# Grouped-query values as eight full-width fp32r products on high and low parts, with the evictions of a step in another order

## The chip, the cores and the metric

The kernel runs on one core of a Trainium2 chip. The metric is the device time of one execution in microseconds; lower is better. All inputs and outputs are float32.

## The reference

One layer of an encoder on 512 tokens of width 1024. Three token mixers work on the same projection of x: neighbourhood attention, grouped-query attention (8 query heads of width 64, 2 key and value heads, each shared by four query heads) and attention into 256 memory tokens. Their outputs are gated, projected, summed and normalised; a mixture of 16 experts follows. What the change touches is the grouped-query branch:

```python
def block(qi):
    s = jnp.einsum('bkgqd,bskd->bkgqs', qi, k, preferred_element_type=jnp.float32) * scale
    p = jax.nn.softmax(s, axis=-1)
    return jnp.einsum('bkgqs,bskd->bqkgd', p.astype(v.dtype), v)
```

for each of four blocks of 128 queries, over all 512 keys.

## The kernel before

In the trace an fp32 product leaves two records, an fp32r product or a transpose one. Where the kernel wants fp32r speed and more than fp32r's precision it splits an operand x into hi = cast(x) and lo = x − hi (`hi_lo`, L99 to L101: a cast on ScalarE, then a subtraction on VectorE that waits for it) and sums the products of the parts. All projection weights go through this: a unit of 128x1024 is loaded, cast (tiles `whi` or `los`) and subtracted (`los`), two units ahead of its use (`Stream.prefetch`).

The grouped-query attention is cut into 16 units: 4 pairs of heads (`hp`) by 4 blocks of 128 tokens (`m`), class `GqaUnit` (L627). A unit goes through five phases:

- `S`: scores of two heads into two PSUM banks (`gs`), two fp32r products each.
- `soft` and `norm`: per head the negated maximum (VectorE), the exponential with its sum (ScalarE); then the reciprocal of the sums and two multiplications (VectorE). The probabilities lie in `att_twin`, two buffers.
- `T`: eight fp32 transposes of 128x128 into two banks (`gt`).
- `tev`: the transposed probabilities go back to SBUF, one copy on VectorE and one on ScalarE.
- `PV`: the values (`gy`), for each of 4 key chunks and 2 heads an fp32 product whose stationary operand is 128x64 of `vg` (the value projection) and whose moving operand is 128 columns. The two heads write the two halves of the partitions, so they lie in different 64-column tiles of the array.
- `yev`: the result is split by `hi_lo` into `yg`.

`Attn.step` (L778) runs three units at once, in this order on each engine:

```python
u.S(); a.T(); b.PV()
u.soft(); a.tev(); u.norm(); b.yev()
```

with u the newest unit, a the one before and b the one before that. On TensorE the transposes of unit a thus stand right behind the scores of unit u and need a's normalisation, which was issued a step earlier. The banks: two for scores, two for transposes, one for values, and three (tag `mm`) that all projections share.

Steps are woven into the projections by `run`: after each piece of a projection one step is issued, then one entry of the background list `bg`, then the eviction of the piece. In the stretch at hand the pieces are the gates of the memory branch (`gate_piece`, 24 products of 512 columns, evicted by a tanh on ScalarE), its projection (`proj_piece`, 12 products, tile `pr`, evicted on VectorE into `macc`) and the neighbourhood values (`nv`, two steps for each of four chunks). `bg` holds the rotary embedding of the queries (`rope_stages`, L386): a square on ScalarE, sums and a reciprocal root on VectorE (L401, L402, L104 to L109), two multiplications (L406, L407), four operations on GpSimd, and transposes of the queries (`rT`) with a cast and a subtraction for each head (`qs`, L446, L447). Engines work in order: what waits holds back all that is queued behind it on that engine.

Of the kernel before, what the change touches and what calls it, by code (L numbers as in the profile page):

```python
# [10 lines left out]
F32R = mybir.dt.float32r  # L11
# [7 lines left out]
P = 128  # L19
# [53 lines left out]
def layer_kernel(ctx: ExitStack, tc: tile.TileContext, xt, xn, first0, wu, bgate, rpb, gains, wrt,  # L73
# [260 lines left out]
    ST = {}  # L334

    def g_mem():
        zz = R("Q3", [P, 4, 1024], "mkvzs")
# [116 lines left out]
    def g_gqa():  # L454
# [3 lines left out]
        b1t = b01[:, 2:4]  # L458
        vg = b1t[:, 0, :512].rearrange("p (m f) -> p m f", m=NT)
        ST.update(khh=kk[:, 0:2], klo=kk[:, 2:4], vg=vg, qs=(qs[:, 0:4], qs[:, 4:8]),  # L460
                  rope=(vs_t[:, 0], b1t[:, 1]), zr=b01[:, 0:2])
        rope = []
        for q in range(3):
            us = ws.take(2)
            zs = ST["A5" if q % 2 else "A6"][:, 1, :512 if q == 0 else 1024].rearrange("p (m c) -> p m c", m=NT)
            for m in range(NT):
                acc = PB("mm", f"gq{q}{m}")
                n_chunk(acc[:, :256], us, xh, xl, m)
                ws.prefetch(2 if m == NT - 1 else 1)
                yield  # L470
                if q == 0:
                    nc.scalar.copy(zs[:, m], acc[:, :P])
                    nc.scalar.copy(vg[:, m], acc[:, P:256])
                else:
                    nc.scalar.copy(zs[:, m], acc[:, :256])
            rope.append(rope_stages(q, zs, 2 if q == 0 else 4, 1 if q == 0 else 0))
            bg.extend(rope[q] if q == 0 else rope[q][:4] if q == 1 else [])
# [105 lines left out]
    class MemUnit:  # L583
# [38 lines left out]
        def yev(self):  # L622
            yh, yl = ST["y2"]
            d = (slice(None), slice(2 * self.hp, 2 * self.hp + 2), slice(self.m * P, (self.m + 1) * P))
            hi_lo(yh[d], yl[d], self.y)

    class GqaUnit:  # L627
        def __init__(self, hp, m):
            self.hp, self.m = hp, m

        def S(self):
# [9 lines left out]

        def soft(self):
            self.p = twin("P").rearrange("p (h c) -> p h c", h=2)
            self.sm = small([P, 2], "sm")
            nm = small([P, 2], "nm")
            for h in range(2):
                nc.vector.tensor_reduce(nm[:, h:h + 1], self.s[h], axis=AX.X, op=ALU.max, negate=True)  # L647
                nc.scalar.activation(self.p[:, h], self.s[h], AF.Exp, bias=nm[:, h:h + 1],  # L648
                                     accum_out=self.sm[:, h:h + 1])

        def norm(self):
            recip_norm(self.p, self.sm, lambda h: self.p[:, h])

# [8 lines left out]
        def tev(self):  # L662
            self.pt = twin("PT").rearrange("p (h k c) -> p h k c", h=2, k=4)
            nc.vector.tensor_copy(self.pt[:, 0], self.t[0])
            nc.scalar.copy(self.pt[:, 1], self.t[1])

        def PV(self):
            self.y = PB("Y", f"gy{self.hp}{self.m}")
            kvh = self.hp // 2
            for kc in range(4):  # L670
                for h in range(2):
                    nc.tensor.matmul(self.y[h * 64:h * 64 + 64, :P], ST["vg"][:, kc, kvh * 64:kvh * 64 + 64],
                                     self.pt[:, h, kc], start=(kc == 0), stop=(kc == 3))

        def yev(self):
            yh, yl = ST["y1"]
            d = (slice(None), self.hp, slice(self.m * P, (self.m + 1) * P))
            hi_lo(yh[d], yl[d], self.y[:, :P])

# [89 lines left out]
    class Attn:  # L769
# [7 lines left out]
        def step(self):  # L777
# [8 lines left out]
            if b:  # L786
                b.PV()
            if u:
                u.soft()
# [4 lines left out]
            if b:  # L794
                b.yev()
            self.pipe = [u, a]
            return True

# [89 lines left out]
    run(g_gqa(), 0.85)  # L888
    at.drain()
    dump("ymh", ST["y2"][0].bitcast(F32))  # L890
    yg = R("Q2", [P, 8, S], "yg", F32R)
# [992 lines left out]
```

## Time and profile before

| what | value |
|---|---|
| median of 3 runs | 959.69 us (959.56 to 962.3) |
| the profiled execution | span 958.0 us from the first to the last instruction; the median of the runs is 1.69 us above it |
| TensorE (PE) busy | 934.3 us, 98% |
| VectorE (DVE) busy | 440.3 us, 46% |
| ScalarE (ACT) busy | 285.8 us, 30% |
| GpSimd (POOL) busy | 97.3 us, 10% |
| granted TensorE clock | 1.00 in the stretches looked at |
| DMA | 251.18 MB, mean 262 GB/s |

The table's busy times are shares of a run with several stages. PE is pipelined: a matmul's record lasts longer than the distance to the next one's start, so the cost of a product is read from starts, not from durations. The same holds, to a lesser degree, for consecutive operations on DVE and ACT.

### The profile page before, as it was taken

The page shows a single profiled execution, that of the slowest core. Times are in us where ns is not written, and L with a number is a line of the kernel's source. Part 1 is how long each engine was busy: PE and PEld are TensorE (multiplying, and loading weights), DVE is VectorE, ACT ScalarE, POOL GpSimd, SP SyncE. Part 2 cuts the span into 40 slices and gives each one's busy share as a digit, 9 for nine tenths or more (in the row PEclk, how much of TensorE's full clock was granted, in tenths as well). Part 3 has the DMA queues.
Part 4 walks back from the last instruction along what each step waited for, and adds up shares of the span by engine and source line. Part 5 has one row for each costly group of instructions (what it writes and reads, how often), then busy time and mean ns, then how long its engine had stood idle before and what let it go on. Part 6 is the DMA issues. An engine that isn't in the chain of part 4 may idle for free. (4 is left out here: it accounts for less than half of the span.)

```text
span 958.0 us, 12971 instructions
## 1 busy us (share of the span) xinstructions
PE 934.3 (98%) x5258; PEld 609.5 (64%) x5258; DVE 440.3 (46%) x840; ACT 285.8 (30%) x560; POOL 97.3 (10%) x112
## 2 busy tenths in 40 slices
PE   9999999999999999999999999999999998998997
PEld 9899878888888888888886433533353333533335
DVE  6347668764376567237464111563232222322426
ACT  6334453543344454333232111110110100110123
POOL 0102303000122231000024004000000000000004
PEclk9999999999999999999999999999999999999999
DMA  9322221211433322566929999999999999999992
GB/s 361 115 67 67 66 67 44 67 47 65 116 85 110 103 83 66 199 252 262 382 73 384 427 423 426 427 433 428 432 429 430 432 428 433 430 430 432 428 422 115
DMA packets 40807, 251.18 MB, mean 262 GB/s; under 512 B 13198, under 2 KB 13582, under 8 KB 25516
## 3 DMA queue, kind: packets, MB, share of 16 engines
q1 hardware_dynamic: 40604, 250.10, 65.1%
q8 instruction: 41, 0.67, 0.3%
q10 hardware_dynamic: 144, 0.26, 0.1%
q14 instruction: 18, 0.15, 0.0%
HBM read 247.46 MB, written 2.10 MB: 260 GB/s over the span
## 5 line engine op out<-in xcount | busy, mean ns | idle before, releaser
L1322 PE MATMUL g<-w,xs 128*64 128x512 f32 x508 | 132.6, 600 | 10.3 <-DMA w<-in_wx 10.2
L1322 PE MATMUL u<-w,xs 128*64 128x512 f32 x508 | 130.6, 592 | 0.0
L1358 PE MATMUL y<-w,hT 128*64 128x512 f32 x480 | 106.0, 593 | 0.0
L1322 PEld LDWEIGHTS u<-w,xs 128*64 128x64 f32 x508 | 36.5, 137 | 72.5 <-issue 72.2
L101 DVE TENSOR_TENSOR y<-y,y 64x512 fp32r<-64x512 f32 x28 | 19.3, 689 | 135.0 <-ACT y L100 135.0
L1322 PEld LDWEIGHTS g<-w,xs 128*64 128x64 f32 x508 | 32.9, 136 | 74.7 <-issue 52.6
L101 DVE TENSOR_TENSOR los<-raw_twin,whi 128x1024 fp32r<-128x1024 f32 x42 | 53.6, 1278 | 57.9 <-ACT whi L100 57.7
L1358 PEld LDWEIGHTS y<-w,hT 128*64 128x64 f32 x480 | 34.2, 137 | 68.1 <-issue 65.1
L286 PE MATMUL gate<-xh,los 128*128 128x512 f32 x192 | 74.9, 390 | 0.0
L1454 DVE TENSOR_TENSOR acc<-acc,cb 128x512 f32<-128x512 f32 x56 | 34.7, 681 | 56.6 <-PE cb L1452 56.6
L284 PE MATMUL gate<-xh,whi 128*128 128x512 f32 x144 | 57.2, 397 | 0.0
L285 PE MATMUL gate<-xl,whi 128*128 128x512 f32 x144 | 56.1, 390 | 0.0
L100 ACT CAST y<-y 64x512 fp32r<-64x512 f32 x28 | 16.2, 579 | 130.5 <-PE y L1358 120.0
L100 ACT CAST whi<-raw_twin 128x1024 fp32r<-128x1024 f32 x42 | 44.1, 1050 | 10.0 <-PE wo L1120 6.5
L1534 POOL TENSOR_TENSOR acc<-acc,ln2g 128x512 f32<-128x512 f32 x8 | 10.0, 1273 | 353.2 <-ACT y L100 352.8
L286 PEld LDWEIGHTS gate<-xh,los 128*128 128x128 f32 x192 | 36.0, 188 | 7.7
L648 ACT ACTIVATE att_twin<-gs,nm 128x512 f32<-128x512 f32 x32 | 21.7, 684 | 49.9 <-DVE nm L647 49.9
L1333 DVE SCALAR_TENSOR_TENSOR tg<-tg,g 128x512 f32<-128x512 f32 x16 | 11.0, 687 | 53.4 <-ACT tg L1332 53.4
L1345 ACT COPY hT<-ht 128x512 f32<-128x512 f32 x15 | 8.8, 586 | 89.2 <-PE ht L1340 89.2
L1332 ACT ACTIVATE tg<-g 128x512 f32<-128x512 f32 x16 | 9.6, 597 | 83.5 <-PE g L1322 78.1
L101 DVE TENSOR_TENSOR los<-raw_twin,los 128x1024 fp32r<-128x1024 f32 x20 | 25.0, 1248 | 19.6 <-ACT los L100 19.5
L284 PEld LDWEIGHTS gate<-xh,whi 128*128 128x128 f32 x144 | 27.0, 188 | 6.6 <-issue 1.2
(458 smaller groups left out, 1898.3 us busy)
## 6 DMA issues: line engine op xcount, KB each, us to landing
w<-in_wx SPq DMA_DIRECT2D x74, 2048.0 KB
w<-in_wx SPq DMA_DIRECT2D x43, 1024.0 KB
raw_twin<-in_wu SPq DMA_DIRECT2D x65, 512.0 KB
raw<-in_wu SPq DMA_DIRECT2D x8, 512.0 KB
xr<-in_xt SPq DMA_DIRECT2D x4, 512.0 KB
macc<-in_xn SPq DMA_DIRECT2D x2, 1024.0 KB
out<-acc SPq DMA_DIRECT2D x7, 256.0 KB
first<-in_first SPq DMA_DIRECT2D x4, 384.0 KB
```

The lines of the kernel that those rows point to most:

```text
L100: nc.scalar.copy(hi, src)
L101: nc.vector.tensor_tensor(lo, src, hi.bitcast(F32), op=ALU.subtract)
L284: nc.tensor.matmul(acc, w_h, rh[:, k], start=(k == 0), stop=False)
L285: nc.tensor.matmul(acc, w_h, rl[:, k], start=False, stop=False)
L286: nc.tensor.matmul(acc, w_l, rh[:, k], start=False, stop=(k == nk - 1))
L648: nc.scalar.activation(self.p[:, h], self.s[h], AF.Exp, bias=nm[:, h:h + 1], accum_out=self.sm[:, h:h + 1])
L1322: nc.tensor.matmul(GU[e][b][hf * 64:hf * 64 + 64], xs, w[b][hf] if isinstance(w[b], list) else w[b][:, hf * 512:hf * 512 + 512], start=(k ...
L1332: nc.scalar.activation(th, g, AF.Tanh, scale=0.5)
L1333: nc.vector.scalar_tensor_tensor(th, th, 1.0, g, op0=ALU.add, op1=ALU.mult)
L1358: nc.tensor.matmul(y[o * 64:o * 64 + 64], hT[:, c, hf * 64:hf * 64 + 64], w[j][:, o * 512:(o + 1) * 512], start=(k == 0 and j == 0), stop= ...
L1454: nc.vector.tensor_tensor(a, a, cb, op=ALU.add)
L1534: nc.gpsimd.tensor_tensor(x, x, g2[:, None, quarters[q]].to_broadcast([P, 2, 256]), op=ALU.mult)
```

## The change

1. `vg` becomes fp32r with a high and a low part side by side: 64 columns of high and 64 of low for each value head and key chunk, in a tile of its own (tag `gb`). The value projection's copy becomes a `hi_lo`.
2. `tev` writes the transposed probabilities as a high and a low part (`gpt`, in place of the twin buffers): two casts on ScalarE and two subtractions on VectorE, in place of one copy on each.
3. `PV` is eight fp32r products: 4 key chunks by high and low probabilities, the stationary operand 128x128 (both parts of the values), the moving one 256 columns (both heads). Partitions 0 to 63 of the result hold what the high values give, 64 to 127 what the low values give.
4. `low` is new: ScalarE copies the lower half (64x256) to SBUF (`glow`), VectorE adds it to the upper half, head by head, into spare columns of the same bank. `yev` reads these.
5. `norm` moves one of the two multiplications to ScalarE (a Copy with a per-partition scale), and both for the first pair of heads (hp 0).
6. The probabilities have one buffer in place of two. For grouped-query units the order behind the products is now: maxima of u, casts of a, first exponential of u, low part of b, second exponential and normalisation of u, eviction of b. The other units keep theirs.

```diff
-        vg = b1t[:, 0, :512].rearrange("p (m f) -> p m f", m=NT)
+        vg = R("gb", [P, NT, 2, 2, 64], "vg", F32R)
...
-                    nc.scalar.copy(vg[:, m], acc[:, P:256])
+                    hi_lo(vg[:, m, :, 0], vg[:, m, :, 1], acc[:, P:256].rearrange("p (g f) -> p g f", g=2))
...
+    GQ = {}
+
     class GqaUnit:
...
+            if not GQ:
+                GQ["p"] = ST["b01"][:, 2]
+                GQ["pt"] = R("Q7", [P, 2, 2, 1024], "gpt", F32R)
+                GQ["low"] = R("bf", [P, 3, 256], "glow")
+            self.i = m
...
-        def soft(self):
...
+        def top(self):
+            self.nm = small([P, 2], "nm")
             for h in range(2):
-                nc.vector.tensor_reduce(nm[:, h:h + 1], self.s[h], axis=AX.X, op=ALU.max, negate=True)
-                nc.scalar.activation(self.p[:, h], self.s[h], AF.Exp, bias=nm[:, h:h + 1],
-                                     accum_out=self.sm[:, h:h + 1])
+                nc.vector.tensor_reduce(self.nm[:, h:h + 1], self.s[h], axis=AX.X, op=ALU.max, negate=True)
+
+        def exp(self, h):
...
+            nc.scalar.activation(self.p[:, h], self.s[h], AF.Exp, bias=self.nm[:, h:h + 1],
+                                 accum_out=self.sm[:, h:h + 1])
 
         def norm(self):
-            recip_norm(self.p, self.sm, lambda h: self.p[:, h])
+            rc = small([P, 2], "rc")
+            nc.vector.reciprocal(rc, self.sm)
+            for h in range(2):
+                if h or not self.hp:
+                    nc.scalar.activation(self.p[:, h], self.p[:, h], AF.Copy, scale=rc[:, h:h + 1])
+                else:
+                    nc.vector.tensor_scalar(self.p[:, h], self.p[:, h], rc[:, h:h + 1], None, op0=ALU.mult)
...
         def tev(self):
-            self.pt = twin("PT").rearrange("p (h k c) -> p h k c", h=2, k=4)
-            nc.vector.tensor_copy(self.pt[:, 0], self.t[0])
-            nc.scalar.copy(self.pt[:, 1], self.t[1])
+            self.pt = [GQ["pt"][:, self.i % 2, j].rearrange("p (h k c) -> p h k c", h=2, k=4) for j in range(2)]
+            for h in range(2):
+                hi_lo(self.pt[0][:, h], self.pt[1][:, h], self.t[h])
 
         def PV(self):
-            self.y = PB("Y", f"gy{self.hp}{self.m}")
-            kvh = self.hp // 2
+            y = PB("Y", f"gy{self.hp}{self.m}", (P, 4, P))
+            self.y = y[:, :2]
+            self.ys = y[:, 2]
             for kc in range(4):
-                for h in range(2):
-                    nc.tensor.matmul(self.y[h * 64:h * 64 + 64, :P], ST["vg"][:, kc, kvh * 64:kvh * 64 + 64],
-                                     self.pt[:, h, kc], start=(kc == 0), stop=(kc == 3))
+                v = ST["vg"][:, kc, self.hp // 2].rearrange("p a f -> p (a f)")
+                for j in range(2):
+                    nc.tensor.matmul(self.y, v, self.pt[j][:, :, kc], start=(kc == 0 and j == 0), stop=(kc == 3 and j == 1))
+
+        def low(self):
+            low = GQ["low"][64:, self.i % 3].rearrange("p (h c) -> p h c", h=2)
+            nc.scalar.copy(low, self.y[64:])
+            for h in range(2):
+                nc.vector.tensor_tensor(self.ys[h * 64:h * 64 + 64], self.y[:64, h], low[:, h], op=ALU.add)
...
-            hi_lo(yh[d], yl[d], self.y[:, :P])
+            hi_lo(yh[d], yl[d], self.ys)
+
+        @staticmethod
+        def behind(u, a, b):
+            if u:
+                u.top()
+            if a:
+                a.tev()
+            if u:
+                u.exp(0)
+            if b:
+                b.low()
+            if u:
+                u.exp(1)
+                u.norm()
+            if b:
+                b.yev()
```

Two places of the order that results. The first is ScalarE around a plain step, that of the twelfth unit, with the tanh and the weight cast that stand ahead of it (`gs` are scores, `gt` transposed probabilities, `gy` values). Before:

```order
L505 ACTIVATE th_1807<-gate_1812,consts 128x512
L100 CAST whi_1877<-raw_twin 128x1024
L648 ACTIVATE att_twin,sm<-gs_1894,nm 128x512
L648 ACTIVATE att_twin,sm<-gs_1897,nm 128x512
L665 COPY att_twin<-gt_1905 128x512
L100 CAST yg<-gy_1910 128x128
```

and with the change:

```order
L510 ACTIVATE th_1856<-gate_1861,consts 128x512
L100 CAST whi_1931<-raw_twin 128x1024
L100 CAST gpt<-gt_1954 128x512
L100 CAST gpt<-gt_1959 128x512
L663 ACTIVATE ropevg,sm<-gs_1948,nm 128x512
L699 COPY glow<-gy_1964 64x256
L663 ACTIVATE ropevg,sm<-gs_1951,nm 128x512
L671 ACTIVATE ropevg<-ropevg,rc 128x512
L100 CAST yg<-gy_1964 128x128
```

The two casts come ahead of the exponentials, the low copy between them, and a normalisation stands between the second exponential and the cast of `yg`.

The second is VectorE in the step of the third unit, ahead of the rotary sums (`ss`). Before:

```order
L101 TENSOR_TENSOR los<-raw_twin,whi_1269 128x1024
L647 TENSOR_REDUCE nm<-gs_1298 128x1
L647 TENSOR_REDUCE nm<-gs_1301 128x1
L664 COPY att_twin<-gt_1304 128x512
L579 RECIPROCAL rc<-sm 128x2
L581 TENSOR_SCALAR att_twin<-att_twin,rc 128x512 x2
L101 TENSOR_TENSOR yg<-gy_1314,yg 128x128
L401 TENSOR_REDUCE ss_1072<-ropesq 128x16
```

and with the change:

```order
L101 TENSOR_TENSOR los<-raw_twin,whi_1278 128x1024
L657 TENSOR_REDUCE nm<-gs_1307 128x1
L657 TENSOR_REDUCE nm<-gs_1310 128x1
L101 TENSOR_TENSOR gpt<-gt_1313,gpt 128x512
L101 TENSOR_TENSOR gpt<-gt_1318,gpt 128x512
L701 TENSOR_TENSOR gy_1323<-gy_1323,glow 64x128 x2
L668 RECIPROCAL rc<-sm 128x2
L101 TENSOR_TENSOR yg<-gy_1323,yg 128x128
L406 TENSOR_REDUCE ss_1077<-ropesq 128x16
```

Two subtractions replace a copy, two additions stand ahead of the reciprocal, and the two multiplications are gone to ScalarE; the rotary sums still stand behind the subtraction of `yg`. On TensorE the order of products is as before, and the order on GpSimd and on SyncE's queue does not change.

## Rows read from the trace of the kernel before

**Rows 1.** The page's busy times of each engine.

```profile
PE 934.3 (98%) x5258; PEld 609.5 (64%) x5258; DVE 440.3 (46%) x840; ACT 285.8 (30%) x560; POOL 97.3 (10%) x112
```

**Rows 2.** Stretches: length, then PE, PEld, DVE, ACT, POOL busy, clock, DMA share, GB/s.

```profile
124.90:240.70 115.80, 115.80 (x750) 94.73 (x750) 81.24 (x154) 54.07 (x123) 9.44 (x6) 1.00 0.17 55
520.00:958.00 438.00, 419.96 (x2229) 172.93 (x2225) 131.48 (x262) 66.12 (x127) 20.61 (x20) 1.00 0.97 411
```

**Rows 3.** Timeline of PE, a plain step: start, length, engine, line, operation, count.

```profile
202.69 0.39 PE L638 MATMUL gs<-kk,qs 128*128 128x512 f32 x1
...
203.60 1.04 PE L659 MATMUL gt<-ident,att_twin 128*128 128x128 f32 x8
204.57 1.09 PE L672 MATMUL gy<-att_twin,ropevg 128*64 128x128 f32 x16
205.59 0.50 PE L284 MATMUL pr<-ym,los 128*128 128x512 f32 x1
...
208.48 0.39 PE L638 MATMUL gs<-kk,qs 128*128 128x512 f32 x1
```

**Rows 4.** Timeline of PE in the memory stage: transposes, then 256-column fp32r products.

```profile
62.84 0.60 PE L608 MATMUL mt<-ident,att_twin 128*128 128x128 f32 x4
63.19 0.36 PE L306 MATMUL gq<-whi,xh 128*128 128x256 f32 x1
63.39 0.28 PE L307 MATMUL gq<-los,xh 128*128 128x256 f32 x1
63.51 0.28 PE L308 MATMUL gq<-whi,xl 128*128 128x256 f32 x1
```

**Rows 5.** Timeline of ACT in the same plain step.

```profile
204.13 0.69 ACT L648 ACTIVATE att_twin<-gs,nm 128x512 f32<-128x512 f32 x1 [2.18 <-DVE nm L647]
...
204.81 0.68 ACT L648 ACTIVATE att_twin<-gs,nm 128x512 f32<-128x512 f32 x1
...
205.47 0.58 ACT L665 COPY att_twin<-gt 128x512 f32<-128x512 f32 x1
205.94 0.28 ACT L100 CAST yg<-gy 128x128 fp32r<-128x128 f32 x1
```

**Rows 6.** Timeline of DVE in the same plain step.

```profile
203.34 1.29 DVE L647 TENSOR_REDUCE nm<-gs 128x1 f32<-128x512 f32 x2
204.55 0.68 DVE L664 COPY att_twin<-gt 128x512 f32<-128x512 f32 x1
205.61 0.17 DVE L579 RECIPROCAL rc<-sm 128x2 f32<-128x2 f32 x1 [0.38 <-ACT att_twin L648]
205.81 0.88 DVE L581 TENSOR_SCALAR att_twin<-att_twin,rc 128x512 f32<-128x512 f32 x2
206.61 0.28 DVE L101 TENSOR_TENSOR yg<-gy,yg 128x128 fp32r<-128x128 f32 x1
```

**Rows 7.** Group of a Copy with per-partition scale on ACT: total, mean ns, idle before.

```profile
L1581 ACT ACTIVATE acc<-fin,l2y 128x512 f32<-128x512 f32 x4 | 2.5, 684 | 0.8 <-PE fin L1565 0.8
```

**Rows 8.** Timeline of DVE, third and fourth unit, around the rotary sums.

```profile
138.27 1.23 DVE L101 TENSOR_TENSOR los<-raw_twin,whi 128x1024 fp32r<-128x1024 f32 x1 [0.95 <-ACT whi L100]
...
143.14 1.21 DVE L401 TENSOR_REDUCE ss<-ropesq 128x16 f32<-128x1024 f32 x1
...
146.57 1.22 DVE L101 TENSOR_TENSOR los<-raw_twin,whi 128x1024 fp32r<-128x1024 f32 x1
147.71 1.28 DVE L647 TENSOR_REDUCE nm<-gs 128x1 f32<-128x512 f32 x2
...
150.16 0.88 DVE L581 TENSOR_SCALAR att_twin<-att_twin,rc 128x512 f32<-128x512 f32 x2
```

**Rows 9.** Timeline of PE: the transposes that need that normalisation.

```profile
151.52 1.03 PE L659 MATMUL gt<-ident,att_twin 128*128 128x128 f32 x8
```

**Rows 10.** Timeline of DVE: eviction of a projection behind the transposed queries.

```profile
181.74 0.69 DVE L533 SCALAR_TENSOR_TENSOR macc<-th,pr 128x512 f32<-128x512 f32 x1
```

**Rows 11.** Timeline of PE: the gate that uses that eviction's bank.

```profile
182.82 0.50 PE L284 MATMUL gate<-xh,whi 128*128 128x512 f32 x1
```

More of the change, by code (lines that the diff above doesn't have):

```diff
@@ L334, in layer_kernel, with att_anew @@
     ST = {}
+    def att_anew():
+        for k in ("P", "PT"):
+            twins.pop(k, None)
+        att.clear()
     def g_mem():
@@ L640, in S @@
                 self.s.append(s)
-        def soft(self):
-            self.p = twin("P").rearrange("p (h c) -> p h c", h=2)
-            self.sm = small([P, 2], "sm")
-            nm = small([P, 2], "nm")
+        def top(self):
+            self.nm = small([P, 2], "nm")
             for h in range(2):
-                nc.vector.tensor_reduce(nm[:, h:h + 1], self.s[h], axis=AX.X, op=ALU.max, negate=True)
-                nc.scalar.activation(self.p[:, h], self.s[h], AF.Exp, bias=nm[:, h:h + 1],
-                                     accum_out=self.sm[:, h:h + 1])
-        def norm(self):
-            recip_norm(self.p, self.sm, lambda h: self.p[:, h])
+                nc.vector.tensor_reduce(self.nm[:, h:h + 1], self.s[h], axis=AX.X, op=ALU.max, negate=True)
+        def exp(self, h):
+            if not h:
+                self.p = GQ["p"].rearrange("p (h c) -> p h c", h=2)
+                self.sm = small([P, 2], "sm")
+            nc.scalar.activation(self.p[:, h], self.s[h], AF.Exp, bias=self.nm[:, h:h + 1],
+                                 accum_out=self.sm[:, h:h + 1])
+        def norm(self):
+            rc = small([P, 2], "rc")
[5 more added lines that the diff above has]
+                    nc.vector.tensor_scalar(self.p[:, h], self.p[:, h], rc[:, h:h + 1], None, op0=ALU.mult)
         def T(self):
@@ L787, in step, with behind @@
                 b.PV()
+            behind = getattr(u or a or b, "behind", self.behind)
+            behind(u, a, b)
+            self.pipe = [u, a]
+            return True
+        @staticmethod
+        def behind(u, a, b):
             if u:
@@ L795, in step @@
                 b.yev()
-            self.pipe = [u, a]
-            return True
         def drain(self):
@@ L889, in layer_kernel @@
     at.drain()
+    att_anew()
     dump("ymh", ST["y2"][0].bitcast(F32))
```

## The prediction

> **What bounds the kernel now.** I read the page's busy times first [rows 1]: TensorE (PE) is busy 934.3 of 958.0 us. Two stretches then say what a change in the grouped-query stage is worth [rows 2]. From 124.9 to 240.7 us, where its steps run, PE is busy for all 115.80 us at full clock; VectorE (DVE) is busy 81.24, ScalarE (ACT) 54.07. So PE sets the pace there, with no visible slack. From 520 us to the end the DMA engines are busy 97%, streaming expert weights into buffers that earlier PE work frees; a shift made at 240 us moves that stream's start and arrives at the end one for one. The sum below is thus made in the stage alone.
>
> **A step on PE.** In a plain step [rows 3] the four score products (gs) take 203.60−202.69 = 0.91, so 0.227 each; eight transposes (gt) 0.97; the values (gy) 1.02; twelve products of pr 2.89; from one step to the next 5.79.
>
> **What the values cost, old and new.** The old values are sixteen records in 1.02 us. The transposes behind them need 0.86, not 0.97: elsewhere four of them take 63.39−0.12−62.84 = 0.43 when full-width products follow [rows 4]. And twelve pr products at 0.227 would take 2.72, not 2.89. So going into and out of 64-column tiles costs 0.11 ahead and 0.17 behind, besides what lies inside the 1.02. The new values are eight products of 256 columns in fp32r on the whole array. The nearest rows are the gq products, same shape and type, one every 0.12 us [rows 4], so 0.96, and no switch on either side. New step: 0.91+0.86+0.96+2.72 = 5.45 against 5.79: **−0.34 a step, and with 16 steps −5.4 us**. Bounds of a product: 0.108, the pitch of a transpose [rows 4] (−6.9 in all), and 0.12 with the 0.17 at each end kept (0). I take 0.12.
>
> A rule speaks against it. The Trainium skill's page TensorEngine Tiling (Array Packing), in "The Solution" and "When to Use Tiling", says that a stationary operand of 64 columns lets two tiles work at once, up to twice as fast; this change gives that up. The trace agrees: sixteen records at 0.107 one behind another would be 1.7 us, and gy takes 1.02. By the rule alone the streaming gets no faster: sixteen pitches of 0.107 in pairs are 0.86, against 0.96 now.
>
> **What ACT and DVE get.** Per step ACT gains one cast of 128x512 (0.47 from start to start, 205.47 to 205.94 [rows 5]), the low copy (0.25, between that and the 0.15 of a 128-column cast) and one or two normalisations with a per-partition scale. Of the last the nearest row is a Copy with such a scale, 0.684 [rows 7]; I take 0.69, and 0.58 from start to start; bounds 0.58 (a plain copy) and 0.88 (the pair on DVE [rows 6]). DVE loses one or both normalisations (0.40 each), swaps a 0.60 copy for two subtractions (1.2) and gains two low additions. For these no row has the shape; I take 0.28 and 0.05 between them, from the 128x128 subtraction [rows 6]; bounds 0.20 and 0.68.
>
> The length of the chain matters more than the load. Today, from the first score product: reductions at +0.65, reciprocal at +2.9, normalised at +4.0 (206.69) [rows 6], the next transposes at 5.79+0.91 = +6.70; slack 2.7. In the new order the two casts stand ahead (from +1.55, when the first transposes are done, to +2.5), then exponential (0.67), low copy (0.25), exponential with its accumulator (0.80): +4.2. On DVE reductions end at +1.86, subtractions at +3.4, the additions wait for the low copy and end at +4.2. Reciprocal +4.4, normalised at +5.1; transposes wanted at 5.45+0.91 = +6.36. Slack 1.2: nothing lost in a plain step.
>
> The end of a step moves from +3.25 on ACT (205.94 [rows 5]) to +5.0, and everything queued behind it goes with it: tanh, the weight casts, the casts of transposed queries (qs), and on DVE, in order, the weights' low parts (los) and the next reductions. Four places have no room.
>
> *The step after a gate, 0.1 each.* Behind +5.0 stand the yg cast (0.15), tanh (0.58), the weight cast (1.1) and los (1.2): it ends at +8.05, that is +2.6 of the next step. Reductions 1.2, subtractions 1.2, additions 0.6, reciprocal 0.2, normalisation 0.69: +6.45, wanted +6.36.
>
> *The rotary step, 4.2.* Its chain now starts with a los at 138.27 [rows 8] behind the qs casts. The step before has two normalisations on ACT and ends at +5.3 instead of +3.25, so los ends 2.1 later and reductions start at 141.5. Then 1.2+1.2+0.6+0.2 to 144.7, two normalisations to 145.9 (transposes 0.3 late), yg cast and subtraction to 146.4, the rotary sums from 143.14 to 146.57, 3.43 long, to 149.85, los 1.14 to 151.0, reductions to reciprocal 3.2 to 154.2, first normalisation 154.95. Today that normalisation ends at 150.16+0.88 = 151.04 and the transposes start at 151.52 [rows 8, 9], slack 0.5; two cheaper values and the 0.3 put them at 151.1. **They wait 3.9; with the 0.3, 4.2 us.**
>
> *The two steps with transposed queries, 2.3.* Today the eviction of pr ends at 181.74+0.69 = 182.43 [rows 10], and the gate that needs its bank starts at 182.82 [rows 11], 0.4 spare. Reductions come some 1.5 later (1.75 for the end of the step before, less an estimated 0.2 that the qs casts wait for PE today), reductions to normalised takes 3.9 instead of 206.69−203.34 = 3.35, so the eviction is 2.1 later, while PE is 0.6 earlier: 2.1+0.6−0.4.
>
> *The value steps, 1.3.* One has two weight casts and two los ahead of its reductions: 0.1−0.58+1.14 = 0.7 late, carried into the next for another 0.3; and 0.3 for the step in which GpSimd's rotary work slows DVE's normalisation.
>
> Other edits: the value projection's copies become pairs (four more subtractions of 128x128, 0.28 each) under a stage in which PE is busy all the time; new tiles and the order of GpSimd and SyncE change nothing there: nothing.
>
> **Sum.** Waits 0.1×4+4.2+2.3+1.3 = 8.2, values −5.4: +2.8 on the profiled span of 958.0, 960.8; the median of the runs stands 1.7 above that span, so **962.5 us**.
>
> **Rivals.**
> 1. *Only the rotary chain waits* (−5.4+4.2 = −1.2, 958.5). The other places are late by 1.1 or less on paper, so shorter additions or a faster low copy empty them. Against: in the pair of query steps the spare is 0.4 today and the chain grows in each part. 0.22.
> 2. *Faster: the casts ahead free the evictions* (954.3). DVE and ACT stay ahead everywhere, as today. It decides in one place: the chain from the third unit's reductions to the fourth's normalisation (13.5 long by the sum) has to shrink below about 9.6, which takes overlap that no row shows. With half of that, 956.4. For it: DVE has 34.6 us idle in the stage [rows 2]. 0.10.
> 3. *The values get no cheaper*: two separate blocks of 128 columns in one product, and the switch paid anyway. Steps stay 5.8 long, which shortens each wait by 0.3 or more (some 6.5 left); with the 0.10 a step of the paired tiles 0.1×16+6.5 = +8, 967.8. Against: rows of the same shape at 0.12. The rule on column tiles points this way. 0.08.
> 4. *The extra operations are dearer* (additions 0.68, normalisation 0.88): each chain 0.9 longer, seven late places, +6 more, 968.5. 0.06.
>
> **Numbers.** The forecast has 0.54, with 960.5 to 965.5 as its own range. About 0.3% (2.9 us) is what a measurement of this kernel can tell from no change; the forecast stands just under that, 962.6, so a little under half of it counts as slower and the rest as the same. Slower: 0.26 of the forecast and rivals 3 and 4: 0.40. Faster: rival 2: 0.10. Same: the rest, 0.50. The range 957.0 to 966.0 leaves out most of 2, 3 and 4, some 0.2.
>
> **What would show it.** gy at 0.12 a product with gt at 0.86 and pr at 2.72 behind it: the −0.34. PE idle about 4 us ahead of the fourth unit's transposes, near 151 us, ended by ACT's normalisation. A wait of 1 us or so ahead of the memory branch's seventh gate (g=2, j=6). DVE solid from 141 to 160 us. I am wrong if PE shows no wait in this stretch (then 954), if gy takes over 1.2 us, or if the shift at 240 us isn't the one at the end.

## The result and the profile after

The changed kernel takes **967.75 us** (median of 4 runs, 967.21 to 969.43) against 959.94 before (4 runs): a ratio of 1.0079, 95% interval 1.0065 to 1.0093. It is 7.8 us slower. The forecast was 962.5, at most 966.0: the sign of the sum was right, its size was not.

The profiled execution has a span of 965.4 us. The page's busy times:

```profile
PE 934.1 (97%) x5130; PEld 610.5 (63%) x5130; DVE 451.6 (47%) x872; ACT 315.9 (33%) x612; POOL 98.3 (10%) x112
```

and two stretches (length, PE, PEld, DVE, ACT, POOL busy, clock, DMA share, GB/s):

```profile
124.90:245.40 120.50, 112.74 (x609) 93.94 (x608) 90.73 (x179) 83.39 (x173) 9.31 (x6) 0.99 0.16 53
520.00:965.40 445.40, 427.60 (x2288) 177.09 (x2288) 134.50 (x275) 66.93 (x129) 21.31 (x21) 0.99 0.97 410
```

Against [rows 1] PE is as busy as before, ACT 30 us busier. In the stage of the change PE now stands idle for 120.50 − 112.74 = 7.8 us, where [rows 2] had none. From 520 us on the stream of weights runs at 97% as before: the shift passes through, as forecast.

The stage can be measured by itself, from the first score product to the last value product. PE's rows that bound it, before (124.97 to 236.64, 111.67 us):

```profile
124.97 0.39 PE L638 MATMUL gs<-kk,qs 128*128 128x512 f32 x1
...
236.64 1.09 PE L672 MATMUL gy<-att_twin,ropevg 128*64 128x128 f32 x16
```

and after (124.93 to 244.45, 119.52 us):

```profile
124.93 0.39 PE L650 MATMUL gs<-kk,qs 128*128 128x512 f32 x1
...
244.45 1.12 PE L695 MATMUL gy<-gpt,vg 128*128 128x256 f32 x8
```

The stage is 7.85 longer, the runs 7.81. This length is used for every experiment below.

**A plain step got cheaper**, nearly as forecast. PE, a plain step of the changed kernel:

```profile
209.13 0.39 PE L650 MATMUL gs<-kk,qs 128*128 128x512 f32 x1
...
210.04 1.03 PE L680 MATMUL gt<-ident,ropevg 128*128 128x128 f32 x8
210.83 1.20 PE L695 MATMUL gy<-gpt,vg 128*128 128x256 f32 x8
211.87 0.40 PE L284 MATMUL pr<-ym,los 128*128 128x512 f32 x1
...
214.62 0.39 PE L650 MATMUL gs<-kk,qs 128*128 128x512 f32 x1
```

5.49 from step to step instead of 5.79 [rows 3]. The values themselves gained nothing (211.87 − 210.83 = 1.04 against 1.02); the transposes ahead went from 0.97 to 0.79 and the products behind from 2.89 to 2.75. So the gain lies at the two edges, as argued; e2 below, which puts the old products behind the new evictions, has 0.97 (205.16 to 206.13) and 2.89 (207.15 to 210.04) back. The old products differ from the new in the width of their tiles and in their number type (fp32 for fp32r), and no run separates the two.

**Three places lost more than that.** VectorE and ScalarE around the fourth unit, whose chain begins with the low part of a weight:

```profile
150.09 1.22 DVE L101 TENSOR_TENSOR los<-raw_twin,whi 128x1024 fp32r<-128x1024 f32 x1
151.22 1.28 DVE L657 TENSOR_REDUCE nm<-gs 128x1 f32<-128x512 f32 x2
152.42 1.27 DVE L101 TENSOR_TENSOR gpt<-gt,gpt 128x512 fp32r<-128x512 f32 x2
153.73 0.62 DVE L701 TENSOR_TENSOR gy<-gy,glow 64x128 f32<-64x128 f32 x2
154.38 0.17 DVE L668 RECIPROCAL rc<-sm 128x2 f32<-128x2 f32 x1
156.10 0.29 DVE L101 TENSOR_TENSOR yg<-gy,yg 128x128 fp32r<-128x128 f32 x1 [1.55 <-ACT yg L100]
```

```profile
152.80 0.37 ACT L699 COPY glow<-gy 64x256 f32<-64x256 f32 x1
...
154.58 1.33 ACT L671 ACTIVATE ropevg<-ropevg,rc 128x512 f32<-128x512 f32 x2 [0.61 <-DVE rc L668]
```

and PE in the same place; in brackets the idle time ahead and its releaser:

```profile
152.83 0.50 PE L650 MATMUL gs<-kk,qs 128*128 128x512 f32 x1 [2.01 <-ACT ropevg L663]
153.17 0.40 PE L651 MATMUL gs<-kk,qs 128*128 128x512 f32 x1
154.02 0.50 PE L650 MATMUL gs<-kk,qs 128*128 128x512 f32 x1 [0.46 <-ACT ropevg L663]
...
155.35 1.97 PE L680 MATMUL gt<-ident,ropevg 128*128 128x128 f32 x8 [0.51 <-ACT ropevg L671]
156.98 1.62 PE L695 MATMUL gy<-gpt,vg 128*128 128x256 f32 x8
158.43 0.40 PE L284 MATMUL gate<-xh,whi 128*128 128x512 f32 x1
```

The transposes start at 155.35; before at 151.52 [rows 9]. Already the scores wait, which the forecast did not say. They are the fifth unit's: their two banks come free only with the fourth unit's exponentials (L663), and these stand in the same late chain. And the eight transposes take 156.98 − 155.35 = 1.63 instead of 0.79. The stretches say why, in part (length, PE busy, clock, DMA share, GB/s):

```profile
152.00:154.00 2.00, 0.73 (x2) 1.00 0.77 238
154.00:156.00 2.00, 1.47 (x5) 0.63 0.06 25
156.00:158.00 2.00, 2.00 (x12) 0.52 0.00 0
158.00:160.00 2.00, 2.00 (x12) 1.00 0.00 0
```

The granted clock fell to 0.5, the 1.2 GHz level, behind those idle times, and came back to 2.4 GHz at about 158. What that costs is read against the unit before, whose two normalisations are both on ScalarE too and whose transposes run at full clock:

```profile
145.70 1.27 PE L680 MATMUL gt<-ident,ropevg 128*128 128x128 f32 x8 [0.16 <-ACT ropevg L671]
...
147.91 0.39 PE L284 MATMUL pr<-ym,los 128*128 128x512 f32 x1
```

From the start of the transposes to the product behind the values PE takes 147.91 − 145.70 = 2.21 there, since the second four wait for the second normalisation, and 158.43 − 155.35 = 3.08 here. So the clock costs 0.9 us.

Comparing the starts of the same products in the two traces place by place gives the account. "Lost" is by how much the shift grows there:

| term | forecast | lost |
|---|---|---|
| third and fourth unit (rotary) | 4.2 | 0.5 + 4.8 = 5.3, of it 0.9 by the clock |
| the two steps with transposed queries | 2.3 | 3.2 |
| the value steps (208 to 240 us) | 1.3 | 3.1 |
| the values in 16 steps | −5.4 | −4.2 (e1 below) |
| all else | 0.4 | 0.4, the rest to 7.8 |

The idle column undercounts such places. A break costs more than its gap: the score product at 152.83 is followed by the next after 0.34, not 0.23, and the last one ahead of a gap lasts its whole record of 0.40, so 0.17 of draining counts as busy.

### The profile page after: what moved, and what is told of

It is laid out like the page before. It is cut to its first block, busy times and chain, and to the rows that moved or that the text cites. A ratio compares the mean times of both kernels' runs of the same rounds, so it can differ in the third digit from the quotient of the medians.

```text
span 965.4 us, 12816 instructions
## 1 busy us (share of the span) xinstructions
PE 934.1 (97%) x5130; PEld 610.5 (63%) x5130; DVE 451.6 (47%) x872; ACT 315.9 (33%) x612; POOL 98.3 (10%) x112
## 5 line engine op out<-in xcount | busy, mean ns | idle before, releaser
L285 PEld LDWEIGHTS gate<-xl,whi 128*128 128x128 f32 x144 | 27.1, 188 | 5.3
```

Source lines behind the costliest of these rows:

```text
L285: nc.tensor.matmul(acc, w_h, rl[:, k], start=False, stop=False)
```

## The experiments

### What each run gave

The length of the stage less that of before (111.67), and the times; before had 959.9 to 960.2 beside each of them:

| run | stage | median | ratio, 95% |
|---|---|---|---|
| the change | +7.85 | 967.75 | 1.0079 (1.0065 to 1.0093) |
| e1 products alone | −4.22 | 956.57 | 0.9971 (0.9958 to 0.9984) |
| e2 evictions alone | +9.22 | 968.83 | 1.0089 (1.0074 to 1.0104) |
| e3 normalisation on VectorE | +1.91 | 962.56 | 1.0026 (1.0011 to 1.0041) |
| e4 no rotary root | +5.76 | 965.88 | 1.0058 (1.0042 to 1.0075) |
| e5 = e3 without low block | −2.18 | 957.85 | 0.9992 (0.9966 to 1.0018) |
| e6 old order | +37.92 | 997.17 | 1.0386 (1.0354 to 1.0417) |
| e7 = e3, root and low parts on GpSimd | +1.66 | 960.70 | 1.0000 (0.9989 to 1.0011) |
| e8 = e3, root on GpSimd | +1.36 | 960.83 | 1.0010 (0.9996 to 1.0023) |
| e9 = e7, three places relieved | −2.58 | 957.48 | 0.9968 (0.9956 to 0.9981) |

### The products apart from the evictions (e1, e2)

```diff
# e1, against the changed kernel
... (normalisation: as in e3 below)
-            self.pt = [GQ["pt"][:, self.i % 2, j].rearrange("p (h k c) -> p h k c", h=2, k=4) for j in range(2)]
-            for h in range(2):
-                hi_lo(self.pt[0][:, h], self.pt[1][:, h], self.t[h])
+            hi = GQ["pt"][:, self.i % 2, 0].rearrange("p (h k c) -> p h k c", h=2, k=4)
+            self.pt = [hi, hi]
+            nc.vector.tensor_copy(hi[:, 0], self.t[0])
+            nc.scalar.copy(hi[:, 1], self.t[1])
...
-            hi_lo(yh[d], yl[d], self.ys)
+            hi_lo(yh[d], yl[d], self.y[:, 0])
...
+                u.exp(0)
+                u.exp(1)
...
-                u.exp(0)
-            if b:
-                b.low()
-            if u:
-                u.exp(1)
```

> The new products alone: eight products of 256 columns on the whole array, behind the old evictions and the old order (reductions, both exponentials, one copy of each transposed tile, both normalisations on VectorE, one pair of operations for the result). Left out: the low part of the probabilities (the high part is used twice) and the addition of the two 64-row blocks. Theory A (the products are worth 0.30 us a step, as the trace of the changed kernel shows in its plain step, and nothing else of the change helps): TensorE works through the stage without a wait, the plain step is 5.49 long, and 16 x 0.30 = 4.8 us come off at the end: 955.1. Rival (rival 3 of the prediction in another form: what the step shows is given back before the end, in the weight stream or in the next stage): 959 to 960.5.

Theory A holds in its mechanism: 956.57 is 1.5 above the time it gave, and PE is busy through its whole stage, as this stretch of e1 shows (columns as in the first stretches above):

```profile
124.90:237.00 112.10, 112.10 (x626) 96.63 (x625) 81.48 (x154) 54.20 (x124) 9.44 (x6) 1.00 0.18 57
```

The stage is 4.22 shorter, 0.26 a step and not the 0.30 of a plain one: in several of the sixteen steps the two timelines show the saving at one edge only. In the profiled execution 2.3 us of the gain are given back behind the stage (the last value product is 3.7 earlier, the end 1.4); e5 below gives back 1.6 in the same way, the other kernels at most 0.5. What takes it there stays open.

```diff
# e2, against the changed kernel
-                v = ST["vg"][:, kc, self.hp // 2].rearrange("p a f -> p (a f)")
-                for j in range(2):
-                    nc.tensor.matmul(self.y, v, self.pt[j][:, :, kc], start=(kc == 0 and j == 0), stop=(kc == 3 and j == 1))
+                for h in range(2):
+                    nc.tensor.matmul(y[h * 64:h * 64 + 64, 0], ST["vg"][:, kc, self.hp // 2, 0].bitcast(F32),
+                                     self.pt[0][:, h, kc].bitcast(F32), start=(kc == 0), stop=(kc == 3))
...
-            nc.scalar.copy(low, self.y[64:])
+            nc.scalar.copy(low, self.y[64:, 0:1].to_broadcast([64, 2, P]))
...
-                nc.vector.tensor_tensor(self.ys[h * 64:h * 64 + 64], self.y[:64, h], low[:, h], op=ALU.add)
+                nc.vector.tensor_tensor(self.ys[h * 64:h * 64 + 64], self.y[:64, 0], low[:, h], op=ALU.add)
```

> The new evictions and their order, with the old products (sixteen of 64 columns in fp32 on the high part alone); every eviction of the changed kernel is still issued, but the low additions add the block to itself and not the low block, so the values are without low parts. Theory A (the loss sits in the chain on ScalarE and VectorE, not in the products): the waits of the changed kernel stay, a step 0.30 us longer takes about 0.3 off each of the seven late places, so 12.3 - 2.1 = some 10 us of loss and no gain: 969 to 971. Rival (TensorE itself loses with the new products, by switching or by the fallen clock): close to before, 960 to 962.

968.83, just under theory A's 969; the rival falls. With the old products the evictions cost 9.2 us and TensorE's saving is absent. Together e1 and e2 give −4.2 + 9.2 = 5.0; the changed kernel loses 7.85. That its shorter steps leave each late chain less room fits the waits (PE's idle time in the stage is 5.7 us in e2 and 7.8 in the changed kernel; ahead of the last unit's transposes 0.51 and 1.09), but no run tests it by itself.

### The normalisation on ScalarE (e3)

```diff
# e3, against the changed kernel
-                if h or not self.hp:
-                    nc.scalar.activation(self.p[:, h], self.p[:, h], AF.Copy, scale=rc[:, h:h + 1])
-                else:
-                    nc.vector.tensor_scalar(self.p[:, h], self.p[:, h], rc[:, h:h + 1], None, op0=ALU.mult)
+                nc.vector.tensor_scalar(self.p[:, h], self.p[:, h], rc[:, h:h + 1], None, op0=ALU.mult)
```

> The changed kernel with both normalisations of every unit on VectorE, as before the change. Theory A (two normalisations on ScalarE, 0.71 us each and one behind another, make VectorE stand idle 1.55 us in each step of the first four units, and this lengthens the rotary place): the two steps ahead of the rotary sums end some 0.5 to 1 us earlier, the wait ahead of the fourth unit's transposes shrinks by 2 us or so, and with it the fall of the clock behind it (some 1 us): 962 to 965. Rival (VectorE's own load sets the chain; 0.40 more for each normalisation that comes back to it, in sixteen units): 969 to 971, waits at the seven places longer by 0.1 to 0.4 each.

962.56, theory A. Giving VectorE *more* work takes 5.9 of the 7.85 us out of the stage (5.4 by the medians). By place some 2.7 of the 5.9 are in the rotary place, of it 0.9 by the clock, which stayed at 1.00 in e3; some 1.0 in the steps with transposed queries and some 2.0 in the value steps. Groups of VectorE from 124.9 to 240 us show the mechanism (operation, count | busy, mean ns | idle ahead and its releaser). The changed kernel:

```profile
L452 DVE TENSOR_TENSOR qs<-rT,qs 64x512 fp32r<-64x512 f32 x7 | 4.8, 689 | 5.1 <-ACT qs L451 5.1
L101 DVE TENSOR_TENSOR yg<-gy,yg 128x128 fp32r<-128x128 f32 x13 | 3.8, 291 | 7.7 <-ACT yg L100 7.7
```

and e3:

```profile
L101 DVE TENSOR_TENSOR yg<-gy,yg 128x128 fp32r<-128x128 f32 x15 | 4.3, 284 | 0.3 <-ACT yg L100 0.3
L452 DVE TENSOR_TENSOR qs<-rT,qs 64x512 fp32r<-64x512 f32 x6 | 4.1, 688 | 2.0 <-ACT qs L451 1.9
```

With the normalisation on ScalarE the step crosses the engines twice more: VectorE's reciprocal, ScalarE's normalisation, ScalarE's cast of `yg`, VectorE's subtraction. ScalarE waits for the reciprocal with the `yg` cast, the tanh, the casts of the weights and of the queries behind it, and VectorE then waits for all of these: 7.7 us at `yg` instead of 0.3. Such idle time is no loss where the step has room (before the change VectorE waited 4.8 us at `yg`); in the late places it stands on the chain. ScalarE in the plain step of the changed kernel:

```profile
212.66 0.69 ACT L663 ACTIVATE ropevg<-gs,nm 128x512 f32<-128x512 f32 x1 [0.91 <-DVE nm L657]
...
213.47 0.37 ACT L699 COPY glow<-gy 64x256 f32<-64x256 f32 x1
213.86 0.69 ACT L663 ACTIVATE ropevg<-gs,nm 128x512 f32<-128x512 f32 x1
...
215.31 0.72 ACT L671 ACTIVATE ropevg<-ropevg,rc 128x512 f32<-128x512 f32 x1 [0.67 <-DVE rc L668]
215.94 0.24 ACT L100 CAST yg<-gy 128x128 fp32r<-128x128 f32 x1
```

The same rows size the low copy: the two exponentials start 1.20 apart instead of 0.68 [rows 5], so it takes 0.52 of ScalarE's chain, not 0.25. In the same rows ScalarE stands idle 0.67 for the reciprocal, works 0.72 and only then starts the `yg` cast. e3 takes away the crossings and the length of ScalarE's part together (its normalisation and the wait ahead of it); no run separates the two.

### The rotary sums and the low block (e4, e5)

```diff
# e4, against the changed kernel
         def s2():
+            if q == 2:
+                nc.vector.memset(rs, 1.0)
+                return
```

> The changed kernel without the sums and the root of the rotary stage that falls beside the fourth unit: the scale of these query heads is a constant 1 (their mean square and its root are left out; some 3.4 us of VectorE, in fourteen operations, become one). Theory A (in that one step a chain on VectorE that has lost its slack ends 3.4 us too late): TensorE's waits between 150 and 156 us, 3.8 us before, shrink to 1 or less, the granted clock stays at 1.0 there (1.1 us more), and 963 to 965 is left; 3 to 4 us of waits stay in the query and value steps. Rival (the wait there is set by ScalarE's work, by the score banks or by something else than VectorE's length): 967 to 968.

965.88, between the two and nearer theory A: the stage gains 2.1 of the 3 us and more expected. PE's waits in e4, the two left in that place and a new one:

```profile
152.62 0.50 PE L653 MATMUL gs<-kk,qs 128*128 128x512 f32 x1 [0.46 <-ACT ropevg L666]
...
153.96 1.27 PE L683 MATMUL gt<-ident,ropevg 128*128 128x128 f32 x8 [0.60 <-ACT ropevg L674]
...
179.27 0.66 PE L434 MATMUL rT<-ident,ropevg 128*128 128x128 f32 x4 [0.61 <-ACT th L513]
```

The 2.98 us of waits there became 1.06, and the clock did not fall (1.00 in the same stretches): from the transposes to the gate PE takes 2.20, as in the third unit. But PE, 2.25 us earlier at the transposes of the queries, now meets a tanh that is only 1.4 earlier (0.61): part of what a shorter chain gives in one place is given back in the next.

```diff
# e5, against e3
         def low(self):
-            low = GQ["low"][64:, self.i % 3].rearrange("p (h c) -> p h c", h=2)
-            nc.scalar.copy(low, self.y[64:])
-            for h in range(2):
-                nc.vector.tensor_tensor(self.ys[h * 64:h * 64 + 64], self.y[:64, h], low[:, h], op=ALU.add)
+            pass
...
-            hi_lo(yh[d], yl[d], self.ys)
+            hi_lo(yh[d], yl[d], self.y[:, 0])
```

> The kernel of e3 (all normalisations on VectorE) without the copy of the low block and its two additions; the pair of operations for the result reads the first 128 columns of the product as they are. Left out: the low part of the values. This measures what is left of the loss in e3, which is +1.3 us at the end of the stage with -4.3 of cheaper products in it, so 5.6 of waits. Theory A (0.53 us of ScalarE between the two exponentials and 0.62 of VectorE in every step are what lengthens the chain): most of these waits go, shift at the end of the stage -3 to -4, as in e1, and 956.5 to 958. Rival (the second transposed cast on ScalarE and the two subtractions ahead of the exponentials are what lengthens it, the additions lie in idle time): 960 to 962.5, the wait of 1.0 us ahead of the fourth unit's scores stays.

957.85, theory A, though the interval is wide: nine of its ten runs lie between 956.97 and 959.39, and one of 969.88 is in the interval too. By the stage the low block costs 1.91 + 2.18 = 4.1 us even with all normalisations on VectorE; the edit takes out the copy and the two additions together. The casts and subtractions of two transposed tiles, in the new order, cost the remaining 4.22 − 2.18 = 2.0 against e1's old evictions and old order.

### The order (e6)

```diff
# e6, against the changed kernel
             if u:
                 u.top()
+                u.exp(0)
+                u.exp(1)
             if a:
                 a.tev()
             if u:
-                u.exp(0)
-            if b:
-                b.low()
-            if u:
-                u.exp(1)
                 u.norm()
             if b:
+                b.low()
                 b.yev()
```

> The changed kernel with the order of the evictions as before the change: reductions, both exponentials, then the casts and subtractions of the transposed tiles, the normalisations, the low copy with its additions, and the pair for the result. Theory A (the order is the part of the change that pays, because the score banks and the transposed banks come free only when ScalarE gets to them): ScalarE reaches the casts only behind both exponentials, VectorE the reciprocal only behind the subtractions, and the chain of a step, some 0.65 to the reductions, 2.0 for exponentials, 1.0 for the casts, 0.8 for the last subtraction, 0.2, 0.7 to 1.4 for normalising, 0.4 + 0.6 for the low block and 0.5 for the result, is about as long as 1.3 plain steps: each of sixteen steps loses some 1.8 to 2.4 us, 995 to 1005. Rival (the same work in another order, no engine is full, so little changes): 965 to 971.

997.17 (two runs, 995.18 and 999.16), theory A. The new order, which the forecast did not price by itself, is worth 29 us to these evictions. That includes the clock, which fell to 0.50 in five places of e6; PE's waits by themselves sum to 22.9 us. Groups of PE in e6, 124.9 to 283 us:

```profile
L695 PE MATMUL gy<-gpt,vg 128*128 128x256 f32 x128 | 23.6, 338 | 7.7 <-DVE yg L101 7.7
...
L680 PE MATMUL gt<-ident,ropevg 128*128 128x128 f32 x128 | 18.2, 287 | 13.3 <-DVE ropevg L673 9.4 <-ACT ropevg L671 3.9
```

Now the values wait too, for their one bank.

### A version with the products' gain (e7, e8, e9)

```diff
# e8, against e3; rsqrt_pool is rsqrt with GpSimd's operations
-            nc.vector.tensor_scalar(ss, ss, 1.0 / 64.0, RMS_EPS, op0=ALU.mult, op1=ALU.add)
-            rsqrt(rs, ss, ...)
+            eng, root = (nc.gpsimd, rsqrt_pool) if q == 2 else (nc.vector, rsqrt)
+            eng.tensor_scalar(ss, ss, 1.0 / 64.0, RMS_EPS, op0=ALU.mult, op1=ALU.add)
+            root(rs, ss, ...)
# e7 has also
-            hi_lo(hi, lo, raw)
+            if 20 <= i <= 34:
+                nc.scalar.copy(hi, raw)
+                nc.gpsimd.tensor_tensor(lo, raw, hi.bitcast(F32), op=ALU.subtract)
+            else:
+                hi_lo(hi, lo, raw)
```

> The kernel of e3 with the rotary root beside the fourth unit on GpSimd alone. Theory A: 2.2 us of VectorE's chain go from the one step that has most to lose; the wait there (2.4 us in e3) shrinks to under 1, those of the query and value steps stay: 959.5 to 961.5. Rival (the root on GpSimd ends so late that the multiplications by it hold VectorE up in the following step): 963 to 966.

> An attempt to have both: the kernel of e3, with the rotary root beside the fourth unit (all but the reduction, 13 small operations on VectorE) on GpSimd, and the low parts of the fifteen weight tiles from the 21st on subtracted on GpSimd too (1.22 us each on VectorE). Theory A (VectorE's length in the late places is what is left of the loss): the waits ahead of the fourth unit go, the gate and the value steps lose theirs, the -4.3 of the products comes through: 956 to 958. Rival (GpSimd takes the same data path as VectorE's copies and subtractions or is so much slower that the weights come late): the normalisations of 0.40 grow, or TensorE waits for a low part: 961 to 966.

e8 came out at 960.83, as theory A had it: the fourth unit's wait shrank to 0.24, but the fifth unit's transposes now waited 0.50 and 1.01, since its two normalisations took 3.32 on VectorE beside GpSimd's rotary multiplications. e7 at 960.70, against its theory A (958) and just under its rival's 961. VectorE and GpSimd in e7 show what took e7's gain:

```profile
149.67 3.39 DVE L425 TENSOR_TENSOR mkvzs<-mkvzs,rs 128x1024 f32<-128x1024 f32 x1 [0.25 <-POOL rs L118]
153.10 1.23 DVE L426 TENSOR_TENSOR mkvzs<-mkvzs,consts 128x1024 f32<-128x1024 f32 x1
...
156.04 1.28 DVE L101 TENSOR_TENSOR gpt<-gt,gpt 128x512 fp32r<-128x512 f32 x2
...
158.21 3.24 DVE L684 TENSOR_SCALAR ropevg<-ropevg,rc 128x512 f32<-128x512 f32 x2
```

```profile
149.59 2.39 POOL L197 TENSOR_TENSOR los<-raw_twin,whi 128x1024 fp32r<-128x1024 f32 x1
...
156.96 1.32 POOL L436 TENSOR_TENSOR ropevg<-mkvzs,consts 128x512 f32<-128x512 f32 x1
158.23 1.30 POOL L437 TENSOR_TENSOR ropesq<-mkvzs,consts 128x512 f32<-128x512 f32 x1
```

The first multiplication (L425) took 3.39 where its like (L426) takes 1.23: it began just behind a GpSimd subtraction, and 151.98 − 149.67 + 1.23 = 3.5 is what waiting for that one's end would give. The Trainium skill's page SBUF — State Buffer ("Who interferes with whom") says that a VectorE instruction with two inputs in SBUF, as L425 is, contends with a GpSimd instruction that reads SBUF, over a pair of ports that the two engines share; the 3.39 agrees. The two normalisations took 3.24 beside GpSimd's rotary multiplications instead of 0.88; the subtractions that read PSUM kept their 1.28. These multiplications were on GpSimd before the change too (the two normalisations of that place took 1.95 in e3): what the earlier root changes is when the two meet. Behind the normalisations PE waited 1.58 and 1.01 us, and the clock fell again (0.60 and 0.55 in the stretches from 162 to 166 us).

```diff
# e9, against e7
-            if 20 <= i <= 34:
+            if 20 <= i <= 31 and i != 25:
...
+                if (self.hp, self.m) == (1, 0):
+                    nc.scalar.activation(self.p[:, h], self.p[:, h], AF.Copy, scale=rc[:, h:h + 1])
+                else:
-                nc.vector.tensor_scalar(self.p[:, h], self.p[:, h], rc[:, h:h + 1], None, op0=ALU.mult)
+                    nc.vector.tensor_scalar(self.p[:, h], self.p[:, h], rc[:, h:h + 1], None, op0=ALU.mult)
```

> The kernel of e7 with three places changed by what its trace shows: the low part that ran on GpSimd from 149.59 to 151.98, beside which VectorE's rotary multiplication took 3.39 instead of 1.2, goes back to VectorE; so do those of the last three tiles, for one of which TensorE waited 0.53; and the two normalisations of the fifth unit, which took 3.24 instead of 0.88 beside GpSimd's rotary multiplications, go to ScalarE. Theory A (GpSimd's large elementwise operations stretch VectorE's operations from SBUF to SBUF, and the 2.6 us of waits at 160 us with the fallen clock behind them, 4.1 us of shift in all, come from that): the shift stays at about -1.9 through 170 us, is -3 to -4 at the end of the stage, and the time is 956 to 957.5. Rival (the fifth unit's chain is late for another reason, by the later reductions): a wait of 1 us or more stays ahead of its transposes, 958.5 to 960.5.

957.48, theory A, inside the 956 to 957.5 it gave; the shift at the end against before, 2.6 us, falls a little short of the 3 to 4 it named. The multiplication is back at 1.23 (VectorE in e9):

```profile
151.55 1.23 DVE L425 TENSOR_TENSOR mkvzs<-mkvzs,rs 128x1024 f32<-128x1024 f32 x1 [0.25 <-POOL rs L118]
```

and PE has no wait until 170 us, as this stretch of e9 shows (length, PE busy, clock, DMA share, GB/s):

```profile
150.00:170.00 20.00, 20.00 (x115) 1.00 0.15 45
```

With nothing left out it is 0.32% faster than the kernel before (0.9968, 0.9956 to 0.9981), 10 us faster than the change as it was made.

## Why the prediction was wrong

**Right.** *The values*: eight products at 0.130 for 0.12, and the gain at the edges; −4.2 (e1) for −5.4: a plain step gave 0.30 for the forecast's 0.34, which is half of the difference over sixteen steps, and the other half is that not all sixteen give what a plain one gives (0.26 on average). Rival 3 is out. The Trainium skill's page TensorEngine Tiling (Array Packing), in "When to Use Tiling", speaks for the old column tiles; the trace agrees with it as far as the streaming goes, which got no faster (1.02 to 1.04). *The place*: the longest wait is ahead of the fourth unit, and the chain on VectorE ran as worked out; it gave 151.0, 154.2 and 154.95 for the start of the reductions, the reciprocal's end and the first normalisation's, measured 151.22, 154.55 and 155.30 (154.58 + 0.72). The sign "DVE solid from 141 to 160 us" did not come: VectorE stood idle 1.55 us behind the reciprocal in the third and in the fourth unit, waiting for ScalarE, as the forecast's own chain has it. *Passing through*: the shift in the stage is the one at the end, in all ten kernels to within 1.1 us by the medians (the table); in the profiled executions all but e1 and e5 agree to 0.5. Rival 1 (only the rotary chain waits) is out by 3.2 and 3.1 us elsewhere, rival 2 by the waits as a whole. Rival 4 (968.5) gave nearly the measured time by luck: the operations that it made dearer were not (two additions 0.62 for 0.6, a normalisation 0.72 for 0.69).

**The step that failed** is the pricing of the waits behind the rotary place, above all "The value steps, 1.3": they lost 3.1, the largest miss of the sum. Of the 1.8 too little, 1.2 is the wait ahead of the last unit's transposes, a place that the sum does not have:

```profile
239.84 1.06 PE L680 MATMUL gt<-ident,ropevg 128*128 128x128 f32 x8 [1.09 <-DVE ropevg L673]
```

Behind the last unit no scores of a next one stand ahead of its transposes, so they are wanted 0.91 sooner than the forecast's "+6.36", and a chain that starts behind a `los` has no room. The other 0.6 of these steps I can't assign to one operation. The second part is "The two steps with transposed queries, 2.3", which lost 3.2. The sum priced the gate alone, and its wait came about as forecast (1.03, ended by the subtraction of a `qs`); but ahead of it, in the same step, the scores (0.28 and 0.47) and the transposes had waited already:

```profile
186.85 1.06 PE L680 MATMUL gt<-ident,ropevg 128*128 128x128 f32 x8 [0.51 <-DVE ropevg L673]
...
189.90 0.47 PE L284 MATMUL gate<-xh,whi 128*128 128x512 f32 x1 [1.03 <-DVE qs L452]
```

**The term that was missing** is the clock: the forecast let a wait cost its length, and PE ran at half speed behind it, 0.9 us in the rotary step, where the sum put nothing. With 1.2 less from the values, 1.8 and 0.9 more in these steps, 0.9 from the clock and 0.2 in the rest of the rotary place, the forecast's +2.8 becomes the measured 7.8.

"Low copy (0.25 ...): +4.2" was mis-sized as well, at 0.52, but this cost little. In the late places VectorE sets the pace: in the fourth unit its subtractions run to 152.42 + 1.27 = 153.69 and the additions start at 153.73, when the low copy has been done since 153.17; in five other late steps the order is the same. Only in a step that began on time (scores from 203.64) do the additions wait for the copy, 0.27 us; that step ends on ScalarE at +5.4 for the forecast's +5.0, and still loses nothing. The additions themselves (0.62 a step) are on VectorE's chain everywhere, as forecast; that fits the 4.1 us of the whole low block (e5).

**What was in the sum but not seen** is that one part of the change carries most of its loss. I counted the normalisations on ScalarE where they fall ("two normalisations to 145.9", "yg cast and subtraction to 146.4"; measured 146.26 and 146.73), but nowhere against leaving them on VectorE, and e3 shows 5.9 us for that choice. Had the forecast costed each numbered part of the change by itself, it might have found a move that lengthens the chain and relieves an engine that was idle nearly a third of the stage ([rows 2]: DVE 81.24 of 115.80).

Not settled: how the 5.9 divides between the crossings and the length of the normalisation on ScalarE. The fall of the clock was never tried by itself; e3 and e4, where it did not fall, also changed other things. And what takes back part of the gain behind the stage in e1 and e5 is open.

## What to carry to other kernels

When work moves between two in-order engines, count the crossings of the chain before the busy time: what stands behind the waiting instruction waits too, and here the busier engine that finished its own chain was the faster one. Follow the chain to the last unit as well, where other work than in a plain step stands ahead. Cost a change part by part, so that a part that pays (the products, the order) isn't sold with one that loses (the normalisation). Before work goes to GpSimd, look for operations of VectorE from SBUF to SBUF on the chain beside it: here they took 3.39 for 1.23 and 3.24 for 0.88.

## What the runs showed of the hardware

- The granted clock fell to 0.5 behind idle times of PE of 2.01, 0.46 and 0.51 us with a few products between them (the change), and of 1.96 us in one piece (e6, from 147.4 to 149.35: 0.50 from 149.5 on). Behind 0.46 and 0.60 (e4) and behind 0.50 and 1.01 (e8) it stayed at 1.00.
- VectorE's operations from SBUF to SBUF stretched beside GpSimd from 1.23 to 3.39 and from 0.88 to 3.24 for two, while its operations that read PSUM did not (1.28 for two, e7).
- On GpSimd the subtraction of 128x1024 takes 2.39, against 1.22 on VectorE.
